# Projection tiles in pairs with seven block products in place of eight, all projections ahead of the mLSTM

## The chip, the cores and the metric

The kernel runs on one core of a Trainium2 chip. The metric is the device time of one execution in microseconds (us). Three runs of the kernel before took 1289.82, 1290.22 and 1290.43 us; their median is 1290.22 us.

## The reference

One layer of a decoder: a sequence of 1024 tokens with 1024 channels, float32, two mixers in parallel that share one input projection.

```python
h = _rmsnorm(x, norm_g)
p = jnp.einsum("bsd,dn->bsn", h, w_in.astype(h.dtype))
q, k, v, o_pre, i_pre, f_pre, z_a, glu_in, z_b, ga_pre, gb_pre = jnp.split(p, SPLIT_POINTS, axis=-1)
qk = jax.nn.silu(_causal_dwconv(jnp.concatenate([q, k], axis=-1), conv_qk_w, conv_qk_b))
...
hm = _mlstm(q.reshape(shp), k.reshape(shp), v.reshape(shp), i_pre, f_pre)
hm = hm * lax.rsqrt(jnp.mean(hm * hm, axis=-1, keepdims=True) + EPS)
hm = hm.reshape(b_, s_, D_A) * mhn_g.astype(jnp.float32)
out_a = (jax.nn.sigmoid(o_pre.astype(jnp.float32)) * hm).astype(x.dtype) * jax.nn.silu(z_a)
y_a = jnp.einsum("bsc,cd->bsd", out_a, w_pa.astype(out_a.dtype))
u = glu_in[..., :D_B] * jax.nn.sigmoid(glu_in[..., D_B:])
u = _causal_dwconv(u, dw_w, dw_b)
u = jax.nn.silu(_layernorm(u, ln_g, ln_b)) * jax.nn.silu(z_b)
y_b = jnp.einsum("bsc,cd->bsd", u, w_pb.astype(u.dtype))
merged = jax.nn.sigmoid(ga_pre) * y_a + jax.nn.sigmoid(gb_pre) * y_b
return x + jnp.einsum("bsd,de->bse", merged, w_out.astype(merged.dtype))
```

The convolution of q and k has 4 taps, that of u has 31. The mLSTM has four heads of 256 channels and goes through the tokens in chunks, with a state that one chunk hands to the next. A last RMSNorm over the channels follows.

## The kernel before

**Products.** A float32 operand is split (`split`, L137) into a high part (a cast on ScalarE) and a low part (a subtraction on VectorE), and `mm3` (L152) adds three matmuls: high by high, high by low, low by high. The weights are the stationary operand. A projection tile (`proj`, L229) has 128 channels by 1024 tokens: two halves of 512 tokens, eight steps along the 1024 input channels, three passes, so 48 matmuls of 512 columns. The projections of w_in are 72 such tiles; v has a form of its own (`v_item`, tokens by 256 channels, one item for each head). y_b, y_a are eight tiles each, and the output projection has 768 matmuls of 256 columns.

**Order.** The program is written as a sequence of items, and a scheduler at build time places each engine's instructions in one fixed list, which the engine then works through in order. First comes the normalised, transposed x (`startup`) with the v of head 0. Then for each head its v, q, k, o (output gate), z_a and four tiles of the gated linear unit, `gb` (its sigmoid is the factor) and `ga`. The mLSTM of a head, four chunks of 256 tokens in six stages each, is laid between the matmuls of the head's last eight tiles (`mlstm_events`). Phase 1b has the merge gates (tiles named sg, first the eight of MB0, then the eight of MA0) and z_b. q, k, v and the gates stay in SBUF until the mLSTM has used them.

**The 31-tap convolution and its layer norm.** `glu_a_item` (L335) forms u and then, at a priority lowered by `LATER`, one start and 30 taps on VectorE over 128x1024 (L341, L344), stores the result in `c_dram` and adds it on GpSimd to `s1`, the sum over channel tiles. `ln_mean` multiplies s1 by a column of ones on TensorE (tstat, L654), and `to_row` transposes the result (trow, L660), writes it to DRAM and loads it back spread over 128 partitions (mu). `ln_var` loads each of the eight tiles c from `c_dram` (ct), subtracts mu, squares, and adds on GpSimd to `sv` (L682); `ln_rstd` and `to_row` give rstd. `d` in the loop of sig_item decides after which sg tile each of these is written: the mean after the first eight, the variance with the next ones. z_b then loads each tile c once more (L673), normalises it, takes the SiLU and multiplies.

**Queues.** All DMAs are issued by SyncE (SP), in order; a store that waits for a result holds up the loads behind it.

## Time and profile before

| | us |
|---|---|
| median of 3 runs | 1290.22 |
| span of the profiled execution | 1287.4 |
| TensorE busy in it | 1275.8 |
| VectorE busy | 816.8 |
| ScalarE busy | 456.6 |
| GpSimd busy | 82.0 |

The profiled execution is known by its span, from its first to its last instruction; the median of the runs stands 2.8 us above it, which is taken for what lies around the span. Matmuls overlap, so the time that a stretch takes is read from the chain of work or from starts, and the mean duration of one matmul (some 0.4 us) is longer than its share of the stretch. The same holds for VectorE: rows that follow one another start closer together than they last.

### The profile page before, as it was taken

Reading aid. Unit: us, or ns where it says so; the run is one execution under the profiler, and the core shown is the slowest. Engines: PE = TensorE matmul, PEld = TensorE weight load, DVE = VectorE, ACT = ScalarE, POOL = GpSimd, SP = SyncE. Lnnn points to the kernel's source line nnn. Section 1 sums busy time; section 2 is a strip of 40 time slices with the busy share of each in tenths; the row PEclk is TensorE's granted clock in tenths of the full one; section 3 lists DMA queues with packets and bytes.
Section 4 is the critical chain, followed back from the end, with each engine's and each line's share of the span. In section 5 each row is a group of like instructions: output and inputs, shape, how many; then the busy total and the mean of one; then the engine's idle time right before and its main releaser. Section 6 shows DMA issues by size and latency. Waiting matters only on the chain.

```text
span 1287.4 us, 16051 instructions
## 1 busy us (share of the span) xinstructions
PE 1275.8 (99%) x6636; PEld 1079.1 (84%) x6636; DVE 816.8 (63%) x1008; ACT 456.6 (35%) x626; POOL 82.0 (6%) x122
## 2 busy tenths in 40 slices
PE   8999999999999999999999999999999999999997
PEld 7888889888889888898888888888888888888997
DVE  6783479995499984799964899262155333344433
ACT  5565441345431444423454211141333211212224
POOL 1000000001000100001010001050000000000002
PEclk9999999999999999999999999999999999999999
DMA  7112121211111221212121123464332344333403
GB/s 219 45 48 53 46 58 42 82 50 58 54 54 50 66 70 37 66 41 66 49 74 50 42 90 115 133 227 127 102 98 82 115 144 137 96 99 98 180 18 132
DMA packets 121495, 109.82 MB, mean 85 GB/s; under 512 B 4945, under 2 KB 109769, under 8 KB 121422
## 3 DMA queue, kind: packets, MB, share of 16 engines
q1 hardware_dynamic: 121422, 108.80, 27.7%
q8 instruction: 52, 0.85, 0.3%
q14 instruction: 21, 0.17, 0.0%
HBM read 87.79 MB, written 21.00 MB: 84 GB/s over the span
## 4 chain that ended last, share of the span: by engine, by line
PE 96%; ACT 1%; DVE 1%; POOL 1%; DMA 0%; issue 0%; SPq 0%; POOLq 0%; ACTq 0%
PE sg L158 14%; PE o L158 7%; PE zb L158 7%; PE k L158 7%; PE ya L158 7%; PE q L158 7%; PE ga L158 7%; PE za L158 7%; PE gb L158 7%; PE yb L158 7%; PE v L158 6%; PE out L158 6%; PE sc L158 2%; PE ip L158 1%; PE up L158 1%; PE np L158 1%
## 5 line engine op out<-in xcount | busy, mean ns | idle before, releaser
L344 DVE SCALAR_TENSOR_TENSOR acc<-u,dww,acc 128x1024 f32<-128x1024 f32 x240 | 307.5, 1307 | 2.9
L138 ACT CAST whi<-wraw 128x1024 fp32r<-128x1024 f32 (+1 forms) x104 | 109.1, 1049 | 372.6 <-PE sg L158 110.6
L139 DVE TENSOR_TENSOR wlo<-wraw,whi 128x1024 fp32r<-128x1024 f32 (+1 forms) x104 | 130.8, 1257 | 78.8 <-ACT whi L138 78.4
L158 PE MATMUL sg<-hth,whi 128*128 128x512 f32 x256 | 101.5, 396 | 0.0
L158 PE MATMUL sg<-hth,wlo 128*128 128x512 f32 x256 | 101.5, 396 | 0.0
L158 PE MATMUL sg<-htl,whi 128*128 128x512 f32 x256 | 100.7, 393 | 0.0
L158 PE MATMUL out<-whi,mrg 128*128 128x256 f32 x512 | 90.8, 280 | 0.0
L158 PE MATMUL ya<-oa,whi 128*128 128x512 f32 x256 | 80.4, 395 | 0.0
L158 PE MATMUL yb<-u,whi 128*128 128x512 f32 x256 | 80.0, 394 | 0.0
L158 PEld LDWEIGHTS out<-whi,mrg 128*128 128x128 f32 x512 | 78.6, 189 | 0.0
L158 PE MATMUL v<-whi,hth 128*128 128x256 f32 (+1 forms) x256 | 71.7, 289 | 2.0 <-ACT hth L138 2.0
L158 PE MATMUL out<-wlo,mrg 128*128 128x256 f32 x256 | 72.0, 281 | 0.0
L158 PE MATMUL v<-whi,htl 128*128 128x256 f32 (+1 forms) x256 | 70.0, 282 | 0.4 <-DVE htl L139 0.4
L158 PE MATMUL v<-wlo,hth 128*128 128x256 f32 (+1 forms) x256 | 69.9, 281 | 0.0
L158 PEld LDWEIGHTS sg<-hth,wlo 128*128 128x128 f32 x256 | 48.3, 189 | 11.9
L158 PEld LDWEIGHTS yb<-u,whi 128*128 128x128 f32 x256 | 48.4, 189 | 11.6 <-DVE u L139 0.3
L158 PEld LDWEIGHTS sg<-htl,whi 128*128 128x128 f32 x256 | 48.0, 187 | 11.7
L158 PEld LDWEIGHTS ya<-oa,whi 128*128 128x128 f32 x256 | 48.0, 188 | 11.4
L158 PEld LDWEIGHTS sg<-hth,whi 128*128 128x128 f32 x256 | 48.1, 188 | 11.0
L158 PE MATMUL ga<-hth,whi 128*128 128x512 f32 x128 | 51.3, 401 | 0.0
L158 PE MATMUL za<-hth,whi 128*128 128x512 f32 x128 | 51.2, 400 | 0.0
L158 PE MATMUL gb<-hth,whi 128*128 128x512 f32 x128 | 50.9, 397 | 0.0
(234 smaller groups left out, 2984.7 us busy)
## 6 DMA issues: line engine op xcount, KB each, us to landing
wraw<-in_w_in_dram SPq DMA_DIRECT2D x80, 512.0 KB, 4.1
ct<-c_dram SPq DMA_DIRECT2D x16, 512.0 KB, 4.6
xt<-in_x_dram SPq DMA_DIRECT2D x8, 512.0 KB, 4.2
oa_dram<-ot SPq DMA_DIRECT2D x16, 256.0 KB, 2.1
c_dram<-acc SPq DMA_DIRECT2D x8, 512.0 KB
sgb_dram<-sg_s SPq DMA_DIRECT2D x8, 512.0 KB, 2.6
sga_dram<-sg_s SPq DMA_DIRECT2D x8, 512.0 KB, 3.0
wraw<-in_w_pb_dram SPq DMA_DIRECT2D x8, 512.0 KB, 4.5
```

The costliest lines, as they stand in the source:

```text
L138: ins = nc.scalar.copy(hi, src)
L139: nc.vector.tensor_tensor(lo, src, hi.bitcast(F32), op=ALU.subtract)
L158: nc.tensor.matmul(ps, a, b, start=(first and j == 0), stop=(last and j == len(todo) - 1))
L344: nc.vector.scalar_tensor_tensor(acc, u[:, k:k + S], dw(k, c), acc, op0=ALU.mult, op1=ALU.add)
```

## The change

Two channel tiles (`jobs`, made by `add`) are computed together. With the two tiles, the two halves of the input channels and the two halves of the tokens, their product is a 2x2 by 2x2 block product, and `quad` forms it with seven block products in place of eight. A block product (`product`) is 128 channels by 512 tokens over 512 input channels: 4 steps and 3 passes, 12 matmuls of 512 columns. So a pair has 84 matmuls where two tiles had 96; there are 36 pairs, jobs 4 to 39, and the four v items are jobs 0 to 3. Of the activations the sums are made once (`sums`); of the weights four block sums are made for each pair (`prep`), and the seven factors are split, seven half tiles where there were four. The partial results X, Z, W in PSUM are copied and added in between by ScalarE and VectorE.

All projections come first. Their results, q and k after the convolution, v, the gates, z_b's product (`u_dram`), go to DRAM. The sums over channel tiles for the layer norm are no longer GpSimd additions but DMAs that add to their destination (`accum_op`), issued by GpSimd: to `s1_dram` in DRAM, and to sv in SBUF. `layer_norm` is written beside jobs 34 and 35, z_b follows as jobs 36 to 39. Then comes the mLSTM, two heads at a time, chunk by chunk, which loads q, k, v and the gate of each chunk; the tiles of y_b are laid between its stages, and y_b loads its input as eight tiles from `u_dram` (`u2_tile`). y_b's product goes to DRAM too (m1_dram) and is loaded for the merge. The buffers of the convolution (u twice, acc once) and the pools that follow share memory that earlier ones must first give up.

```diff
-        def fin():
-            nc.sync.dma_start(c_dram[c], acc)
-            if c == 0:
-                nc.gpsimd.tensor_copy(s1, acc)
-            else:
-                nc.gpsimd.tensor_tensor(s1, s1, acc, op=ALU.add)
-
...
+        a11, a12 = pair("a", raw[:, 1:3])
+        sm = [wq.tile([P, 2, 512], F32, tag="sum", name=f"sum{n}_{i}", bufs=2) for i in range(2)]
+        nc.vector.tensor_tensor(sm[0][:, 0], raw[:, 0], raw[:, 3], op=ALU.add)
+        nc.vector.tensor_tensor(sm[0][:, 1], sm[0][:, 0], raw[:, 1], op=ALU.add)
+        yield
+        s1, s2 = pair("t", sm[0], DMA_LOW)
+        nc.vector.tensor_tensor(sm[1][:, 0], raw[:, 0], raw[:, 1], op=ALU.add)
+        nc.vector.tensor_tensor(sm[1][:, 1], sm[0][:, 1], raw[:, 2], op=ALU.add)
+        yield
+        s3, s4 = pair("s", sm[1], DMA_LOW)
+        yield
+        (a22,) = pair("b", raw[:, 3:4])
+        j["w"] = (a11, a12, s1, s2, s3, s4, a22)
...
+    def sums(tp, ext):
+
+        later = []
+        for k in range(4):
+            r = tp.tile([P, 4, 512], F32, tag="r", name=f"tr{k}")
+            nc.vector.tensor_tensor(r, hb[:, :, 0, k, :].bitcast(F32), hb[:, :, 1, k, :].bitcast(F32), op=ALU.add)
+            t1 = tp.tile([P, 512], F32, tag="t1", name=f"t1_{k}", bufs=4)
+            t3 = tp.tile([P, 3, 512], F32, tag="t3", name=f"t3_{k}")
+            nc.vector.tensor_tensor(t1, r[:, 0], r[:, 2], op=ALU.subtract)
+            nc.vector.tensor_tensor(t3[:, 0], r[:, 3], r[:, 2], op=ALU.subtract)
+            nc.vector.scalar_tensor_tensor(t3[:, 1], t1, -1.0, r[:, 3], op0=ALU.mult, op1=ALU.subtract)
+            nc.vector.scalar_tensor_tensor(t3[:, 2], t3[:, 1], -1.0, r[:, 1], op0=ALU.mult, op1=ALU.subtract)
+            split(ext[:, :, 0, k, :], ext[:, :, 1, k, :], t3)
+            later.append(t1)
+            yield
+        for k in range(4):
+            split(hb[:, 2, 0, k, :], hb[:, 2, 1, k, :], later[k])
...
+    def product(ps, a, b, first, last):
+        for k in range(4):
+            for p, q in PASSES:
+                nc.tensor.matmul(ps, a[p][:, k, :], b[:, q, k, :], start=(first and k == 0 and p == 0 and q == 0),
+                                 stop=(k == 3 and p == 1), skip_group_check=True)
+
+    def quad(n, dst, emit):
+
+        j = jobs[n]
+        bank = lambda name: state["qb"].tile([P, 512], F32, tag="qb", name=f"{name}{n}")
+        ext = state["ext"]
+        b11, b21, t1, b22 = (hb[:, i] for i in range(4))
+        t3, t2, t4 = (ext[:, i] for i in range(3))
+        a11, a12, s1, s2, s3, s4, a22 = j["w"]
+        X, Z = bank("x"), bank("z")
+        product(X, a11, b11, True, False)
+        yield
+        nc.scalar.copy(dst(0, 0), X)
+        product(Z, s1, t1, True, False)
+        yield
+        nc.scalar.copy(dst(1, 1), Z)
+        product(X, s2, t2, False, False)
+        yield
+        nc.scalar.copy(dst(0, 1), X)
+        W = bank("w")
+        product(W, a12, b21, True, True)
+        yield
+        nc.vector.tensor_tensor(dst(0, 0), W, dst(0, 0), op=ALU.add)
+        emit(0, 0, dst(0, 0), False)
+        product(X, s3, t3, False, False)
+        yield
+        nc.vector.scalar_tensor_tensor(dst(1, 1), X, -1.0, dst(1, 1), op0=ALU.mult, op1=ALU.subtract)
+        emit(1, 1, dst(1, 1), False)
+        product(Z, s4, b22, False, True)
+        yield
+        nc.vector.tensor_tensor(dst(0, 1), Z, dst(0, 1), op=ALU.add)
+        emit(0, 1, dst(0, 1), False)
+        product(X, a22, t4, False, True)
+        yield
+        emit(1, 0, X, True)
...
+            acc = cv.tile([P, S], F32, tag="acc", name=f"acc{c}", bufs=1)
+            with tc.high_priority(offset=-LATER):
+                nc.vector.tensor_scalar(acc, u[:, 0:S], dw(0, c), db(c), op0=ALU.mult, op1=ALU.add)
+                for k in range(1, KD):
+                    nc.vector.scalar_tensor_tensor(acc, u[:, k:k + S], dw(k, c), acc, op0=ALU.mult, op1=ALU.add)
+                nc.sync.dma_start(c_dram[c], acc)
+                if c == 0:
+                    nc.sync.dma_start(s1_dram, acc)
+                else:
+                    nc.gpsimd.dma_start(s1_dram, acc, accum_op=ALU.add)
...
+        s1 = lnp.tile([P, S], F32, tag="ct", name="s1", bufs=2)
+        nc.sync.dma_start(s1, s1_dram)
+        ps, st = token_stat(s1, 0)
+        nc.vector.tensor_scalar(st, ps, 1.0 / D, None, op0=ALU.mult)
+        yield
+        to_row(st, 0, mu)
+        yield
+        for c in range(KT):
+            ct = centred(c, 0)
+            if c == 0:
+                nc.scalar.activation(sv, ct, AF.Square)
+            else:
+                nc.scalar.activation(ct, ct, AF.Square)
+                nc.gpsimd.dma_start(sv, ct, accum_op=ALU.add)
+            yield
+        ps, st = token_stat(sv, 1)
+        nc.vector.tensor_scalar(st, ps, 1.0 / D, EPS, op0=ALU.mult, op1=ALU.add)
+        nc.gpsimd.tensor_tensor(st, st, half, op=ALU.pow)
+        yield
+        to_row(st, 1, sv)
...
+    for n in range(4, first_zb - 2):
+        run_job(n)
+    close(cv_cm)
+    ln_cm, state["lnp"] = pool("lnp", reuse_waits="tile")
+    ln = layer_norm()
+    for n in range(first_zb - 2, first_zb):
+        run_job(n, ln)
+    for _ in ln:
+        pass
+    for n in range(first_zb, len(jobs)):
+        run_job(n)
...
+        for i in range(len(chunks) + 2):
+            for f in (at(i - 1, "v"), at(i - 1, "u"), at(i + 2, "l"), at(i, "s"), None, at(i, "k"), at(i + 1, "p"), None,
+                      at(i - 2, "f"), None, at(i, "i")):
+                yield f
...
+    def u2_tile(c):
+        ut = u2p.tile([P, 2, S], F32R, name=f"u2_{c}")
+        raw = yp.tile([P, S], F32, tag="st", name=f"ur{c}", bufs=2)
+        nc.sync.dma_start(raw, u_dram[c])
+        split(ut[:, 0, :], ut[:, 1, :], raw)
+        u2.append(ut)
+
+    def y_b():
+        for d in range(KT):
+            sg = yp.tile([P, S], F32, tag="st", name=f"sgb{d}", bufs=2)
+            nc.sync.dma_start(sg, sgb_dram[d])
+            ps = yield from proj(d, f"yb{d}", rhs=lambda k, sl: (u2[k][:, 0, sl], u2[k][:, 1, sl]))
+            nc.vector.tensor_tensor(sg, ps, sg, op=ALU.mult)
+            nc.sync.dma_start(m1_dram[d], sg)
+
+    chunks[0]["l"]()
+    chunks[1]["l"]()
+    do_load(0)
+    chunks[0]["p"]()
+    yb = y_b()
+    ny = 0
+    last = False
+    for i, f in enumerate(stages()):
+        if f is not None:
+            f()
+        elif i > 22:
+            for _ in range(1 if ny % 8 else 1):
+                next(yb, None)
+                if ny % 8 == 0:
+                    ahead(ny // 8, 1)
+                ny += 1
```

Three places show how this moves instructions in the engines' lists. The first is on TensorE, where the sums for the layer norm (tstat) and their transposes (trow) stand. Before, in the list of merge-gate tiles (sg):

```order
L158 MATMUL sg_6566<-hth,whi_6515 128x512
L158 MATMUL sg_6566<-htl,whi_6515 128x512
L158 MATMUL sg_6566<-hth,wlo_6516 128x512
L654 MATMUL tstat_6624<-ones,s_103 128x2 x8
L158 MATMUL sg_6648<-hth,whi_6573 128x512
L158 MATMUL sg_6648<-htl,whi_6573 128x512
L660 MATMUL trow_6642<-ident,tst_6633 8x128
```

The second sum (tstat from sv) stood 280 rows further on, with sg tiles in between. After, z_6315 is a product of job 39 and z_6180 one of job 38:

```order
L398 MATMUL z_6315<-hb,hi39t 128x512 x2
L398 MATMUL z_6315<-hb,lo39t 128x512
L549 MATMUL tstat_5599<-ones,s_5597 128x2 x8
L555 MATMUL trow_5632<-ident,tst_5608 8x128
L549 MATMUL tstat_5864<-ones,sv 128x2 x8
L555 MATMUL trow_5876<-ident,tst_5873 8x128
L398 MATMUL z_6180<-hb,hi38s 128x512 x2
L398 MATMUL z_6180<-hb,lo38s 128x512
```

Both sums now stand directly behind one another, behind job 38's fifth and job 39's second product; behind them come seven products, the rest of z_b's last two jobs.

The second place is on VectorE, where the last tile's convolution ends (acc). Before:

```order
L344 SCALAR_TENSOR_TENSOR acc_6108<-u_6105,dww,acc_6108 128x1024 x7
L139 TENSOR_TENSOR wlo_6516<-wraw_6403,whi_6515 128x1024
L344 SCALAR_TENSOR_TENSOR acc_6108<-u_6105,dww,acc_6108 128x1024 x6
L139 TENSOR_TENSOR wlo_6574<-wraw_6461,whi_6573 128x1024
L139 TENSOR_TENSOR wlo_6656<-wraw_6519,whi_6655 128x1024
L668 TENSOR_SCALAR tst_6633<-tstat_6624 128x8
L662 COPY rw_6644<-trow_6642 8x128
L139 TENSOR_TENSOR wlo_6723<-wraw_6577,whi_6722 128x1024
L674 TENSOR_TENSOR ct_0_6706<-ct_0_6706,mu 128x1024
L674 TENSOR_TENSOR ct_1_6710<-ct_1_6710,mu 128x1024
```

After, with lo39t a low part of job 39's weights:

```order
L103 TENSOR_TENSOR lo39a<-raw_6162,hi39a 128x1024
L500 SCALAR_TENSOR_TENSOR acc_4980<-u_4825,dww,acc_4980 128x1024
L422 TENSOR_TENSOR f_0_6177<-w_6220,f_0_6177 128x512
L103 TENSOR_TENSOR lo39t<-sum_0_6237,hi39t 128x1024
L500 SCALAR_TENSOR_TENSOR acc_4980<-u_4825,dww,acc_4980 128x1024 x12
L576 TENSOR_SCALAR tst_5608<-tstat_5599 128x8
L557 COPY rw_5634<-trow_5632 8x128
L564 TENSOR_TENSOR ct_0_5658<-ct_0_5658,mu 128x1024
L564 TENSOR_TENSOR ct_1_5680<-ct_1_5680,mu 128x1024
L564 TENSOR_TENSOR ct_2_5704<-ct_2_5704,mu 128x1024
```

The last 12 taps and then the statistics now stand behind job 39's second weight split, and no work of another kind lies among the eight subtractions.

The third place is on TensorE at a pair of the gated linear unit (job 21; job 29 reads alike). Before, an item's last matmuls (here of the last ga tile) were followed by the next item's:

```order
L158 MATMUL ga_6034<-hth,wlo_5928 128x512
L158 MATMUL ga_6034<-hth,whi_5927 128x512
L158 MATMUL ga_6034<-htl,whi_5927 128x512
L158 MATMUL ga_6034<-hth,wlo_5928 128x512
L158 MATMUL sg_6156<-hth,whi_6152 128x512
L158 MATMUL sg_6156<-htl,whi_6152 128x512
```

After, x_4052 is a product of job 23, and z_3720 the sixth of job 21's seven:

```order
L398 MATMUL x_4052<-ext,hi23s 128x512 x2
L398 MATMUL x_4052<-ext,lo23s 128x512
L398 MATMUL x_4052<-ext,hi23s 128x512 x2
L398 MATMUL x_4052<-ext,lo23s 128x512
L398 MATMUL x_4052<-ext,hi23s 128x512
L398 MATMUL z_3720<-hb,hi21s 128x512 x2
L398 MATMUL z_3720<-hb,lo21s 128x512
L398 MATMUL z_3720<-hb,hi21s 128x512 x2
```

Job 21's sixth product has been moved behind the seven of job 22 and the first four of job 23. The copy on ScalarE that it waits for writes u_3717, and the buffer of u_3717 is given up by the convolution of channel tile 3; VectorE's list has that convolution's last tap 35 rows behind job 21's first combination (L422).

## Rows read from the trace of the kernel before

**Rows 1.** The page: span, busy time by engine, granted clock in 40 slices.

```profile
span 1287.4 us, 16051 instructions
...
PE 1275.8 (99%) x6636; PEld 1079.1 (84%) x6636; DVE 816.8 (63%) x1008; ACT 456.6 (35%) x626; POOL 82.0 (6%) x122
...
PEclk9999999999999999999999999999999999999999
```

**Rows 2.** The page's chain that ended last, by engine.

```profile
PE 96%; ACT 1%; DVE 1%; POOL 1%; DMA 0%; issue 0%; SPq 0%; POOLq 0%; ACTq 0%
```

**Rows 3.** The chain in order of time: start us, us, what.

```profile
47.84 22.13 PE q L158 x95
...
204.17 22.65 PE v L158 x192
226.82 22.37 PE q L158 x96
...
897.60 1.68 PE tstat L654 x16
...
1011.40 89.17 PE yb L158 x384
1100.57 89.52 PE ya L158 x384
1190.09 70.84 PE out L158 x600
```

**Rows 4.** Busy time in stretches: stretch, us, engines, clock, DMA share, GB/s.

```profile
206.00:383.00 177.00, 177.00 (x943) 150.81 (x942) 142.46 (x175) 70.36 (x96) 10.00 (x19) 1.00 0.20 57
```

**Rows 5.** VectorE in order of time: start us, us, instructions.

```profile
209.97 8.46 DVE L344 SCALAR_TENSOR_TENSOR acc<-u,dww,acc 128x1024 f32<-128x1024 f32 x7
218.34 1.22 DVE L139 TENSOR_TENSOR vl<-v,vh 128x1024 fp32r<-128x1024 f32 x1
219.48 8.46 DVE L344 SCALAR_TENSOR_TENSOR acc<-u,dww,acc 128x1024 f32<-128x1024 f32 x7
...
241.95 4.06 DVE L310 SCALAR_TENSOR_TENSOR qraw<-qpre,par,qraw 128x511 f32<-128x511 f32 x6
245.92 1.28 DVE L344 SCALAR_TENSOR_TENSOR acc<-u,dww,acc 128x1024 f32<-128x1024 f32 x1
...
1111.80 1.29 DVE L753 TENSOR_TENSOR sga<-ya,sga 128x512 f32<-128x512 f32 x2 [8.84 <-PE ya L158]
1113.01 1.28 DVE L754 TENSOR_TENSOR sga<-sga,m 128x512 f32<-128x512 f32 x2
```

**Rows 6.** VectorE, ScalarE and GpSimd around the layer norm's statistics, in order of time.

```profile
830.96 0.28 DVE L662 COPY rw<-trow 8x128 f32<-8x128 f32 x1 [0.52 <-PE trow L660]
...
839.46 2.36 DVE L674 TENSOR_TENSOR ct<-ct,mu 128x1024 f32<-128x1024 f32 x2 [7.09 <-DMA mu<-mu_dram]
...
899.56 2.57 POOL L687 TENSOR_TENSOR tst<-tst,half 128x8 f32<-128x8 f32 x1 [30.41 <-DVE tst L686]
...
919.09 1.28 ACT L714 ACT_TABLE_LOAD   x1 [6.73 <-DVE ct L713]
```

**Rows 7.** The tile ct: durations min/median/max in ns; time to landing of its loads.

```profile
L674 DVE TENSOR_TENSOR ct<-ct,mu x16: 1211/1226/3419, 839.5 to 987.8; 128x1024 f32<-128x1024 f32 x16
...
L714 ACT ACTIVATE ct<-ct,par x8: 1225/1243/1245, 920.4 to 990.4; 128x1024 f32<-128x1024 f32 x8
...
L680 ACT ACTIVATE ct<-ct x7: 1050/1060/1062, 843.5 to 865.5; 128x1024 f32<-128x1024 f32 x7
L682 POOL TENSOR_TENSOR sv<-sv,ct x7: 2395/2407/3267, 844.7 to 866.7; 128x1024 f32<-128x1024 f32 x7
...
DMA to landing us min/median/max: 3.2/4.6/5.3
```

**Rows 8.** Time to landing of the stores of sg_s, 512 KB each.

```profile
DMA to landing us min/median/max: 2.6/2.8/3.2
```

**Rows 9.** The last stretch, as in rows 4; the last matmul ends at 1280.7.

```profile
1286.00:1287.40 1.40, 0.00 (x0) 0.00 (x0) 0.00 (x0) 0.00 (x0) 0.00 (x0) 0.50 0.00 0
```

More of the change, by code (lines that the diff above doesn't have):

```diff
@@ new lines, with token_stat @@
+    for i in range(4):
+        add(f"gb{i}", lambda n: act_job(n, AF.Sigmoid, keep="sg"), GB0_, i)
+        add(f"ga{i}", lambda n, i=i: glu_job(n, 2 * i), GA0_, i)
+        for name, fn, base, h in rest[6 * i:6 * i + 6]:
+            add(f"{name}{h}", fn, base, h)
+    first_zb = len(jobs)
+    for i in range(4):
+        add(f"zb{i}", lambda n, i=i: zb_job(n, i), ZB0, i)
+    def token_stat(acc, n):
+        ps = ms(f"tstat{n}")
+        for t in range(TT):
+            nc.tensor.matmul(ps[:, 2 * t:2 * t + 2], acc[:, t * P:(t + 1) * P], ones, start=True, stop=True)
+        st = state["lnp"].tile([P, TT], F32, name=f"tst{n}")
+        return ps[:, 0:2 * TT].rearrange("p (t o) -> p t o", o=2)[:, :, 0:1].rearrange("p t o -> p (t o)"), st
@@ new lines, in zb_job, with run_job @@
+    def zb_job(n, i):
+        cts = []
+        for j in range(2):
+            ct = centred(2 * i + j, 1)
+            nc.vector.tensor_tensor(ct, ct, state["rstd"], op=ALU.mult)
+            nc.scalar.activation(ct, ct, AF.Silu, bias=lb(2 * i + j), scale=lg(2 * i + j))
+            cts.append(ct)
+        return act_job(n, AF.Silu, store=lambda j: u_dram[2 * i + j], by=lambda j: cts[j])
+    def run_job(n, *others):
+        load(n + 1)
+        side = [prep(n + 1) if n + 1 < len(jobs) else iter(()), *others]
+        for step, _ in enumerate(jobs[n]["fn"](n)):
+            if step > 1:
+                for g in side:
+                    next(g, None)
+        for _ in side[0]:
+            pass
@@ new lines, with start @@
+    st_cm, st_pool = pool("st_pool", reuse_waits="tile")
+    warm = ms("warm")
+    for _ in range(11):
+        nc.tensor.transpose(warm[:, 0:P], ident, ident)
+    state["st"] = st_pool
+    gen = startup(st_pool)
+    def start(t):
+        next(gen, None)
+        if t == 4:
+            load_params(st_pool)
+    state["start"] = start
+    start(0)
+    start(1)
+    run_job(0)
+    close(st_cm)
+    gate_steps = gates()
+    next(gate_steps)
+    run_job(1)
+    next(gate_steps, None)
+    close(vt_cm)
@@ new lines, in do_split, with ahead, proj @@
+    def do_split(i):
+        if i < len(slots) and i not in done:
+            do_load(i)
+            done.add(i)
+            hi, lo = [wpool.tile([P, KT * P], F32R, tag=x, name=f"{x}{i}", bufs=3) for x in ("whi", "wlo")]
+            split(hi, lo, raws.pop(i))
+            splits[i] = (hi, lo)
+    def ahead(i, n):
+        for j in range(i, i + n + 1):
+            do_split(j)
+        do_load(i + n + 1)
+    def proj(i, name, rhs):
+        do_split(i)
+        wv = [v.rearrange("p (k c) -> p k c", k=KT) for v in splits.pop(i)]
+        ps = pj(name)
+        for hf in range(2):
+            sl = slice(hf * 512, (hf + 1) * 512)
+            pairs = [((wv[0][:, k, :], wv[1][:, k, :]), rhs(k, sl)) for k in range(KT)]
+            for k in range(0, KT, 2):
+                mm3(ps[:, sl], pairs[k:k + 2], first=k == 0, last=k == KT - 2)
+                yield
+        return ps
@@ L632, in run @@
+    while todo:
+        oa_tile(todo.pop(0))
     def run(gen, i):
```

693 lines of the change are left out of this document (331 added, 362 removed).

## The prediction

> **What bounds the kernel now.** I read the page first, then the chain, then the stretch of one head. TensorE is busy 99% at full granted clock [rows 1] and holds 96% of the chain that ended last [rows 2]; no other engine has more than 1%. So nothing is waited for, and time is a count of matmuls. The chain in order of time gives the price: 96 matmuls of 512 columns, one q item, take 22.37 us, 0.2331 us each; a v item takes 22.65 [rows 3]. In the stretch of head 1 (an item for v and seven more items, 206 to 383) VectorE is busy 142.5 of 177 us [rows 4]: 80%, the engine that stands next. The layer norm's statistics, a sequence of stalls between VectorE, GpSimd and DMAs, lie beside sg matmuls and cost TensorE 1.7 us [rows 3, 6].
>
> **What is removed.** A product is 12 x 0.2331 = 2.80 us, a pair 84 x 0.2331 = 19.58 for 22.38. 36 pairs save 36 x 2.80 = 100.7 us. On TensorE alone the new program would be:
> - start (the first q chain ends at 69.98, less its 22.38) 47.6;
> - three v items at 22.6: 67.8;
> - 36 pairs: 704.9;
> - the mLSTM, which is what is left of the span: 1287.4 - 47.6 - 36 x 22.38 - 67.8 - (89.17 + 89.52) - 97.3 = 90.3, less 4.5 for the startup's gate transposes and the layer norm's two sums, which I count elsewhere: 86;
> - y_b and y_a 178.7; from the end of y_a (1190.09) to the end of the span 97.3 [rows 3].
>
> This makes 1182, and with about 4 us of waiting for the gates' transposes (VectorE's `sums` now stand ahead of them; estimated as seven VectorE operations at 0.6) 1186. Job 4 then starts at 47.6 + 67.8 + 4 = 119.4.
>
> **VectorE in the pairs.** Its price is read from starts that follow one another: a tap (209.97 to 218.34 for seven) 1.196, a subtraction of 1024 (218.34 to 219.48) 1.14, 512 columns 0.605 (1111.80 to 1113.01 for two), 512 columns of the other form 0.66 (241.95 to 245.92 for six) [rows 5]. A pair's weights take three subtractions of 1024, one of 512 and four sums of 512; its results two combinations of the first form and one of the second: 3.42 + 0.60 + 2.42 + 1.21 + 0.66 = 8.3. Eight jobs (q, k, o, z_a, two glu, two merge gates) take 66.4, two convolutions of 31 taps 74.2, twelve taps for q and k 14.4, two products of gates 2.3, four halves of u 2.4: 159.7 us, where TensorE wants 8 x 19.58 = 156.6. The saving thus uses up VectorE's reserve: it is full, and the convolution, which stands at low priority, is late wherever it is waited for.
>
> **Where that is waited for: two glu pairs.** At job 21 (and 29) the sixth product stands behind a copy into a buffer of u that the convolution of channel tile 3 (5) gives up. VectorE has ahead of it, from job 21's first combination, 21 taps (25.1), six taps of q and k (7.2), five subtractions of 1024 (5.7), twelve operations of 512 (7.2): 45.2, and the copy 0.6. TensorE has 12 products laid between, 33.6. It stands 45.8 - 33.6 = 12.2 us; twice: 25 us in round figures. (At job 13 the same count gives 22 us of VectorE against 25 of TensorE: nothing.) These stalls also pay for VectorE's excess of 3.1 us in each of the 4.25 groups of eight.
>
> **The layer norm, the large term.** 34 pairs and four products of job 38 end at 119.4 + 665.7 + 11.2 + 25 = 821.3. Then VectorE has a combination, a subtraction and the last 12 taps (14.4): the convolution ends at 837.4. TensorE has done its seven products ahead of tstat by 119.4 + 665.7 + 19.6 + 25 = 829.7. There it stands, in its fixed list, and the seven products behind it can't pass. The chain:
> - the DMA that adds to s1. No DMA of this kind is in the trace. Nearest rows: a store of 512 KB lands in 2.6 to 3.2 us [rows 8], a load of ct in 3.2 to 5.3 [rows 7]. An addition has to read and write, so I take a load's median, 4.6; bounds 2.6 (a plain store) and 9.2 (two passes). It ends at 842.0; the load of s1, 4.6, at 846.6;
> - tstat 1.7 [rows 3], its scaling 0.2, trow 0.5; from the copy of the row to the first use of mu 8.5 (830.96 to 839.46) [rows 6]: 857.5;
> - the variance. Before, GpSimd's additions of 2.4 us in SBUF stood here [rows 7]; now DMAs, with two buffers of ct. Two subtractions 2.4, a square 1.06 and an addition 4.6 make 8.1 for the first two tiles; then three rounds of load 4.6 + 1.2 + 1.06 + 4.6 = 11.5: 42.6, ends at 900.1. Bounds: 30 with additions of 2.6 and loads of 3.2; 68 with additions of 9.2, which then follow one another: 12.7 + 6 x 9.2;
> - tstat 1.7, scaling 0.2, GpSimd's power 2.57, trow 0.5, row to rstd 8.5 [rows 6]: 913.6;
> - restart: TensorE's sixth product of job 38 waits for a buffer that z_b's first tile gives up: normalising 1.14, the table load 1.28, SiLU 1.24, a product 1.14, store 2.8, copy 0.6 [rows 5 to 8] = 8.2: 921.8. TensorE has stood 92 us, about as much as the seven-product form saves.
>
> Of that standing the last row shows what follows: with the last matmul at 1280.7 the granted clock from 1286 is 0.50, the lower of the two levels [rows 9]. I add 3 us, one product at half speed. Products: 921.8 + 19.6 + 3 = 944.4.
>
> The Trainium skill, "DMA: Bandwidth & Descriptors", "Anatomy of one DMA — SWDGE (gpsimd) path", gives for a DMA issued by GpSimd 2.0 us plus the bytes over 436 GB/s, by which 512 KB would take an estimated 3.2 us, the loop 37 us, and the sum would be 1322; no run so far shows whether it holds for a DMA that adds.
>
> **After it.** z_b's eight tiles go through two buffers, four rounds of load 4.6 and four passes, about 9 each: the last product's store is ready 36 us behind rstd. In SP's list it stands ahead of the loads of y_b's input (eight, in two buffers: 4.6 + 1.06 + 1.14, four rounds, 27): y_b can begin at 913.6 + 36 + 27 = 977. TensorE has about four mLSTM chunks before that (16 chunks in 86 us: 5.4 each, 22): 944.4 + 22 = 966, so 11 to 12 us are lost. In the rest, TensorE's work of a chunk depends on copies and factors; uncovered, one such pass of ScalarE and one of VectorE (1.06 + 0.6) would cost 27 us over 16 chunks, covered by the other head's chunk and y_b nothing; I take 8.
>
> **The sum.** 944.4 + 86 + 178.7 + 97.3 + 12 + 8 = 1326.4, and 2.8 us by which the median stands above the profiled span: **1329 us**, 3.0% above 1290.22. A measurement of this kernel can tell 0.2% from no change.
>
> **Rivals.**
> - **TensorE stays the bound (faster).** For it: before, the same statistics cost 1.7 us. It needs the convolution to end some 85 us before TensorE reaches tstat; then the 92 + 3 us vanish: 1234 (without the glu stalls and those after it, 1189). Against: VectorE's list holds the last 12 taps directly ahead of the statistics, and the count above gives it no reserve. It decides at an end of the convolution near 745; near 795 it would be equal. Chance 0.10.
> - **VectorE bounds all pairs.** If operations cost what they last (tap 1.28, 1024 columns 1.22, 512 columns 0.64 [rows 5]), eight jobs take 171 against 156.6 plus the glu stalls' share of 5.9: 8.3 x 4.25 = 35 us more, 1364. Against: rows that follow one another do start closer. Chance 0.10.
> - **The mLSTM phase waits throughout**, at its upper bound and with one load's latency more in each pair of chunks: 19 + 8 x 2.6 = 40 more, 1369. Against: two heads take turns. Chance 0.06.
> - **The clock stays low** through all seven products after the stand: 19.6 - 3 more, 1346. The last row shows the fall, no row a recovery. The Trainium skill, "TensorE: Matmul & The Clock Gate", "Part 1: The HAM clock gate", calls half clock the default that activity releases; rows 9 agree with the first half. Chance 0.04.
>
> **How the numbers follow.** The forecast has 0.70. Its cheap end: variance loop 30 (-12), addition to s1 2.6 (-2), one glu stall less (-12), no loss after (-20): 1283. Its dear end: loop 68 (+25), addition to s1 9.2 (+5), the mLSTM's bound (+19): 1378. The range leaves out the first rival and the corner of the cheap end, and takes in the others: 1288 to 1380. Faster: 0.10 from the first rival and 0.04 from the cheap corner; same 0.04; slower 0.82.
>
> **What would show it.** Products at 2.80 us and a pair at 19.6; VectorE over 90% busy until the convolution ends; about 12 us of waiting for a ScalarE copy at jobs 21 and 29, nothing at 13; TensorE idle some 90 us around the two tstat, ended by DMAs that add, VectorE and mu's way through DRAM; a second hole of some 10 us before y_b; TensorE busy near 1180 in all. I am wrong if a DMA that adds takes far from 4.6 us (seven of them stand in a row), if the convolution ends tens of us earlier, or if the mLSTM with y_b between its stages stalls by more than 30 us.

## The result, and the profile after

The changed kernel takes 1388.53 us (median of 4 runs, 1385.22 to 1390.03) where the kernel before took 1290.33 beside it: 1.0759 times, 95% interval 1.0743 to 1.0774. The forecast had the sign and the place of the largest loss, but 1329 us, with a range to 1380. The profiled execution spans 1383.5 us where the sum of the prediction gave 1326.4; this is how the 57.1 us between them lie, each end of a stretch read from TensorE's list in order of time:

| stretch | sum of the prediction | trace | more |
|---|---|---|---|
| start, to job 4 | 119.4 | 123.5 | 4.1 |
| job 4 to the last product ahead of tstat | 710.3 | 721.2 | 10.9 |
| TensorE's stand at the two tstat, to the restart | 92.1 | 95.1 | 3.0 |
| seven products behind it | 22.6 | 22.2 | -0.4 |
| mLSTM with y_b | 195.2 | 217.5 | 22.3 |
| y_a to the end | 186.8 | 204.0 | 17.2 |

Where the 4.1 us at the start come from was not looked for. The page of after, to set beside [rows 1, 2]; the chain's line is short here, since the chain was followed back only to 1032 us:

```profile
span 1383.5 us, 16366 instructions
...
PE 1212.9 (88%) x6204; PEld 1017.5 (74%) x6204; DVE 1031.0 (75%) x1322; ACT 552.0 (40%) x844; POOL 56.5 (4%) x157
...
PEclk9999999999999989999899997557799999899999
...
PE 15%; DMA 3%; DVE 3%; ACT 2%; POOL 1%; issue 1%; SPq 0%; POOLq 0%; ACTq 0%; DVEq 0%
```

TensorE is busy 63 us less and the span is 96 us longer: it no longer sets the time alone. Stretches of after, columns as in [rows 4]:

```profile
123.50:844.70 721.20, 690.17 (x2940) 554.18 (x2940) 657.71 (x691) 299.94 (x389) 6.13 (x12) 0.99 0.31 90
844.70:939.80 95.10, 7.94 (x36) 7.16 (x35) 28.59 (x28) 11.41 (x11) 8.57 (x9) 0.53 0.49 132
939.80:962.00 22.20, 22.20 (x84) 17.67 (x84) 16.93 (x17) 9.76 (x13) 0.00 (x0) 0.87 0.44 145
962.00:1000.00 38.00, 22.52 (x114) 19.49 (x114) 30.81 (x52) 30.14 (x55) 2.44 (x17) 0.73 0.91 292
1000.00:1179.50 179.50, 167.46 (x1009) 145.90 (x1009) 123.06 (x284) 86.43 (x195) 20.34 (x81) 0.99 0.62 196
1179.50:1206.00 26.50, 17.54 (x48) 9.43 (x48) 11.97 (x10) 8.08 (x8) 0.00 (x0) 0.81 0.61 198
```

In the first, the pairs, VectorE is busy 657.7 of 721.2 us (91%, where it had 80% in [rows 4]) and TensorE stands 31 us. The second is the stand. In the fourth, the mLSTM's first 38 us, TensorE works for 22.5 of them at a mean clock of 0.73. TensorE around the stand, in order of time (start, us; in brackets the idle time ahead and what ended it):

```profile
865.80 3.57 PE L549 MATMUL tstat<-ones,s 128*128 128x2 f32 x16 [21.07 <-DMA s<-s_dram]
...
921.27 3.58 PE L549 MATMUL tstat<-ones,sv 128*128 128x2 f32 x16 [51.27 <-DMA sv<-ct]
926.87 0.37 PE L555 MATMUL trow<-ident,tst 128*8 128x128 f32 x1 [2.02 <-POOL tst L590]
939.78 1.22 PE L398 MATMUL z<-hb,hi38s 128*128 128x512 f32 x2 [12.55 <-ACT f L415]
```

And VectorE: the first tap of three convolutions, the weight split ahead of one of them, and the last taps of the last one.

```profile
268.53 1.22 DVE L103 TENSOR_TENSOR lo12a<-raw,hi12a 128x1024 fp32r<-128x1024 f32 x1 [5.61 <-ACT hi12a L102]
271.64 0.81 DVE L498 TENSOR_SCALAR acc<-u,dww,par 128x1024 f32<-128x1024 f32 x1 [1.89 <-DMA s_dram<-acc]
...
623.57 0.81 DVE L498 TENSOR_SCALAR acc<-u,dww,par 128x1024 f32<-128x1024 f32 x1 [7.24 <-DMA s_dram<-acc]
...
797.37 0.81 DVE L498 TENSOR_SCALAR acc<-u,dww,par 128x1024 f32<-128x1024 f32 x1 [7.00 <-DMA s_dram<-acc]
...
840.04 15.81 DVE L500 SCALAR_TENSOR_TENSOR acc<-u,dww,acc 128x1024 f32<-128x1024 f32 x12
```

The last convolution ends at 855.8 (forecast 837.4). A tile's first tap waits for the DMA that adds the tile before it to s1, since acc has one buffer: 18.4 us over four convolutions. At 268.5 and 447.2 VectorE also waited 5.6 and 3.6 us for a cast, as no tap was left in its list between the end of one tile and the first tap of the next: 27.6 us with these. No term of the prediction had either wait.

### The profile page after: what moved, and what is told of

The parts are those of the page before. It is cut to its first block, busy times and chain, and to the rows that moved or that the text cites. A ratio compares the mean times of both kernels' runs of the same rounds, so it can differ in the third digit from the quotient of the medians.

```text
span 1383.5 us, 16366 instructions
## 1 busy us (share of the span) xinstructions
PE 1212.9 (88%) x6204; PEld 1017.5 (74%) x6204; DVE 1031.0 (75%) x1322; ACT 552.0 (40%) x844; POOL 56.5 (4%) x157
## 5 line engine op out<-in xcount | busy, mean ns | idle before, releaser
L112 PE MATMUL v<-hi,hb 128*128 128x256 f32 (+1 forms) x512 | 95.0, 288 | 2.6 <-ACT hb L102 2.1
L112 PEld LDWEIGHTS v<-hi,hb 128*128 128x128 f32 x512 | 79.9, 192 | 3.7 <-ACT hb L102 2.7
L112 PE MATMUL v<-lo,hb 128*128 128x256 f32 (+1 forms) x256 | 71.6, 288 | 0.0
L448 ACT ACTIVATE f<-f 128x512 f32<-128x512 f32 x72 | 45.3, 632 | 57.5 <-DVE f L426 31.6
L470 DVE SCALAR_TENSOR_TENSOR qa<-qr,par,qa 128x1023 f32<-128x1023 f32 (+2 forms) x48 | 60.0, 1276 | 0.0
L102 ACT CAST whi<-wr 128x1024 fp32r<-128x1024 f32 x24 | 25.2, 1049 | 78.1 <-PE ya L112 57.4
L112 PE MATMUL ya<-oa,wlo 128*128 128x512 f32 x128 | 51.5, 402 | 0.0
L112 PE MATMUL yb<-u,wlo 128*128 128x512 f32 x128 | 50.9, 398 | 0.0
L112 PEld LDWEIGHTS out<-wlo,mrg 128*128 128x128 f32 x256 | 49.1, 192 | 0.0
L112 PEld LDWEIGHTS v<-lo,hb 128*128 128x128 f32 x256 | 48.6, 194 | 0.0
```

What stands on the lines that cost most here:

```text
L102: ins = nc.scalar.copy(hi, src)
L112: nc.tensor.matmul(ps, a, b, start=(first and j == 0), stop=(last and j == len(todo) - 1))
L448: nc.scalar.activation(t[j][:, HF[hf]], src, func, scale=sgn(neg))
L470: nc.vector.scalar_tensor_tensor(acc[j][:, s:], raw[j][:, 0:S - s], cw(KQ - 1 - s, t), acc[j][:, s:], op0=ALU.mult, op1=ALU.add)
```

## The experiments

They ran in five groups (e1 to e4, e5 to e8, e9 to e12, e13 to e16, e17 and e18), the kernels of a group on one chip with the kernel before; a ratio is to the kernel before, with its 95% interval.

| run | us | ratio |
|---|---|---|
| the change | 1388.5 | 1.0759 [1.0743, 1.0774] |
| e1_acc2 | 1350.1 | 1.0465 [1.0448, 1.0483] |
| e2_low_by_dma | 1342.1 | 1.0404 [1.0388, 1.0419] |
| e3_eight_products | 1353.1 | 1.0501 [1.0467, 1.0534] |
| e4_oa_buffers | 1381.5 | 1.0713 [1.0697, 1.0729] |
| e5_one_pass | 1340.9 | 1.0393 [1.0376, 1.0411] |
| e6_early_loads | 1350.7 | 1.0467 [1.0451, 1.0483] |
| e7_lows_on_gpsimd | 1358.4 | 1.0527 [1.0511, 1.0543] |
| e8_yb_behind | 1368.5 | 1.0605 [1.0583, 1.0628] |
| e9_one_pass_short | 1301.8 | 1.0090 [1.0072, 1.0108] |
| e10_sums_on_gpsimd | 1378.1 | 1.0681 [1.0659, 1.0703] |
| e11_all_hidden | 1351.2 | 1.0467 [1.0443, 1.0492] |
| e12_low_by_dma_all | 1330.9 | 1.0318 [1.0285, 1.0352] |
| e13_glu_sooner | 1330.3 | 1.0309 [1.0293, 1.0324] |
| e14_glu_sooner_two | 1322.4 | 1.0245 [1.0225, 1.0265] |
| e15_lows_half | 1324.4 | 1.0264 [1.0247, 1.0281] |
| e16_stores_on_gpsimd | 1298.6 | 1.0066 [1.0050, 1.0082] |
| e17_squares_own_buffer | 1295.5 | 1.0038 [1.0025, 1.0051] |
| e18_squares_two_sooner | 1293.4 | 1.0031 [1.0019, 1.0042] |

**What holds the convolution up: its buffer.**

```diff
-            acc = cv.tile([P, S], F32, tag="acc", name=f"acc{c}", bufs=1)
+            acc = cv.tile([P, S], F32, tag="acc", name=f"acc{c}", bufs=2)
```

> The convolution's result gets two buffers (acc, 2 for 1). Theory: VectorE is full and the layer norm's chain begins where the last convolution ends; after's trace shows VectorE idle 1.9, 2.3, 7.2 and 7.0 us at the first tap of a convolution, until the DMA that adds the last result to s1 has landed. Without this wait the last tap ends up to 18 us earlier than 855.8, TensorE's stand of 95 us begins and ends that much earlier or shrinks, and the kernel takes 1370 to 1380 for 1388.5. Rival: VectorE has slack elsewhere or the list only shifts, and the time stays within 3 us of 1388.5.

One buffer more takes 38 us off, twice the most that was expected. TensorE in that run, in order of time:

```profile
826.77 3.58 PE L549 MATMUL tstat<-ones,s 128*128 128x2 f32 x16 [14.34 <-DMA s<-s_dram]
...
882.65 3.58 PE L549 MATMUL tstat<-ones,sv 128*128 128x2 f32 x16 [51.67 <-DMA sv<-ct]
...
901.19 1.22 PE L398 MATMUL z<-hb,hi38s 128*128 128x512 f32 x2 [12.57 <-ACT f L415]
```

The chain from the first tstat on is as it was (74.4 us to the restart, 74.0 in the change). All of the gain lies ahead of it: the last tap ends at 817, TensorE is there at 812.4 for 844.7, and the stalls in jobs 23 and 31 are gone (no wait of more than 1.3 us between job 4 and tstat). In the change they were 7 us each, and what stood there was a buffer of another kind:

```profile
508.91 1.22 PE L398 MATMUL x<-ext,hi23t 128*128 128x512 f32 x2 [7.09 <-ACT qr L412]
```

The copy into qr had waited for the store of a q result, that is for VectorE's taps of q (ScalarE in the change):

```profile
503.14 1.28 ACT L472 ACT_TABLE_LOAD   x1 [5.80 <-DVE qa L470]
...
508.27 0.58 ACT L412 COPY qr<-x 128x512 f32<-128x512 f32 x1 [1.65 <-DMA q_dram<-qa]
```

So VectorE was late in the pairs too, and not only at the end. But the edit does more than end the waits at the first taps: with two buffers the scheduler lays the two convolutions of a pair beside one another, and VectorE's list is another. In e1 the second tile's first tap stands 4.4 us behind the first tile's:

```profile
162.07 0.81 DVE L498 TENSOR_SCALAR acc<-u,dww,par 128x1024 f32<-128x1024 f32 x1
...
166.43 0.81 DVE L498 TENSOR_SCALAR acc<-u,dww,par 128x1024 f32<-128x1024 f32 x1
```

In the change it stands at 271.64, behind all 31 of the first. At job 21's first weight split VectorE has done 93 operations of the convolution in the change and 103 in e1; up to there, and to the first tap behind it, the change had lost 13.4 us between tiles, 4.2 of them at first taps. That the one buffer costs 38 us is shown; how much of it is waiting and how much the order that the buffer forces on the list, no run separates.

**The order alone, and VectorE's load.** e3 forms each pair with eight products: its quad is

```diff
+        for t, hf in ((0, 0), (1, 1), (0, 1), (1, 0)):
+            X = bank(f"x{t}{hf}_")
+            product(X, w[t][0], bb[2 * hf], True, False)
+            yield
+            product(X, w[t][1], bb[2 * hf + 1], False, True)
+            yield
+            nc.scalar.copy(dst(t, hf), X)
+            emit(t, hf, dst(t, hf), False)
```

without the sums of weights and activations.

> The order of the change alone: each pair by eight block products as before (96 matmuls for 84), no sums of activations or weights, results copied by ScalarE. Theory: TensorE has 36 x 2.80 = 101 us more, VectorE per pair some 5 us less, so the convolution keeps ahead, the 95 us at the tstat and the 31 us of stalls in the pairs go, and what the order costs is left: the waits in the mLSTM with y_b (about 42 us over the matmuls) and ahead of y_a (15): 1340 to 1350, that is 50 to 60 more than before. Rival: the stand at tstat belongs to the order (all projections first), not to VectorE's load: 1430 or more.

It takes 1353.1, 8 us over the middle of what was expected: all of the change but the seven products costs 63 us, and these add 35 to that. The stalls in the pairs go, but not the whole stand: the two tstat still wait 9.5 and 14.7 us. VectorE between 297 and 471, e3 and then the change:

```profile
297.00:471.00 174.00, 174.00 (x770) 144.06 (x769) 115.67 (x105) 65.05 (x91) 1.97 (x4) 1.00 0.31 91
```

```profile
297.00:471.00 174.00, 170.73 (x736) 137.08 (x735) 164.81 (x174) 74.03 (x97) 2.19 (x4) 1.00 0.34 97
```

66% busy against 95%, and TensorE without a gap against 3.3 us of gaps. Beside e1, which has two acc buffers, the seven products seem to bring 3 us of their 101 (1350.1 to 1353.1), but the two intervals overlap, and eight products with two buffers were not run.

e2 sets the kernel's switch `DMA_LOW`, by which ScalarE and an adding DMA form two of four low parts:

> Two of a pair's four weight splits form their low part with ScalarE and a DMA that adds (the switch DMA_LOW that the kernel has), which takes 2 x 1.14 = 2.3 us per pair off VectorE, 78 us in 34 pairs. Theory (VectorE full, convolution late): the convolution ends near 780, the stalls in jobs 23 and 31 go, the stand at the two tstat falls from 95 to some 55 us, and the kernel takes 1300 to 1330. Rival: such a DMA takes 5.4 to 6.0 us in after's trace, so weights come late for their product and TensorE waits in every pair: 1380 or more.

1342.1: 46 us less, not 58 or more as expected. The last tap ends at 798.8, but TensorE waits some 18 us in the pairs, most of it for combinations that VectorE does late, and later once for such a DMA itself. VectorE in turn waits 13.8 us for acc, which has one buffer here, and 53.6 us over the whole run for buffers of sums that such DMAs still read. One wait of TensorE of either kind:

```profile
426.06 1.22 PE L398 MATMUL x<-ext,hi18b 128*128 128x512 f32 x2 [2.95 <-DVE f L426]
...
851.96 0.80 PE L398 MATMUL z<-hb,lo39t 128*128 128x512 f32 x1 [7.51 <-DMA lo39t<-sum]
```

**The chain of the layer norm.** e5 takes the variance from sums of squares, so the second pass goes:

```diff
+                sq = u[:, 0:S]
+                nc.scalar.activation(sq, acc, AF.Square)
...
+                    nc.gpsimd.dma_start(s2_dram, sq, accum_op=ALU.add)
```

> On top of the two acc buffers (1350.1 us): the variance is taken as mean of squares less squared mean. ScalarE squares each convolution's result as soon as it is there (into the buffer of u that it frees), a DMA adds it to a second sum, and the second pass over the eight stored tiles goes. Theory: the stand at the two tstat (826.8 to 901.2 in that run) is a chain of latencies, 55 us of it the loop of load, subtraction, square and adding DMA; without the loop the restart comes 45 to 55 us earlier and the time is 1295 to 1305. Rival: the kernel is bound elsewhere meanwhile (y_b's input, z_b's tiles), so part of the gain is given back: 1310 to 1335.

1340.9, above even what the rival named. From the last tap to the restart it takes 38 us for 84, as the theory had it; but the last tap is at 857.8 again, because u is held until its squares are added, and TensorE waits at the copies into u, in jobs 13, 21 and 29, three waits of 4.9 to 9.1 us and two shorter ones. The longest:

```profile
661.16 1.22 PE L399 MATMUL x<-ext,hi29t 128*128 128x512 f32 x2 [9.06 <-ACT u L413]
```

This is the kind of stall that the prediction had counted for the change, and it appears when it is u that is short. Place and size agree in part: jobs 21 and 29 lose 7.8 and 12.5 us, where 12.2 each were counted, but at the sixth product only 5.0 and 3.5 of them, and job 13, where nothing was counted, loses 4.9. e9 squares the first six tiles on GpSimd in quarters, in a buffer of its own (and has e4's buffers):

> On top of the two acc buffers (1350.1 us): the single pass for the variance again, but the squares no longer hold a buffer of u: for the first six tiles GpSimd squares quarters in a buffer of their own, only the last two tiles use u. Also the three buffers for y_a's loads (worth 7 us). Theory: in the run before, the chain behind the last tap fell from 84 to 38 us, and 42 us were lost ahead of it because u was held; with u free both gains stay: 1350 - 46 - 7 = 1297, range 1290 to 1305. Rival: squares on GpSimd beside VectorE slow the taps, which are the bound: 1315 or more.

1301.8, inside the range and 5 us over the sum. Both gains stay: TensorE is at tstat at 819 and restarts at 860.0. GpSimd's squares, 26.0 us in all, leave the taps at 1286 ns on average, so the rival's condition did not come.

**Ahead of y_a.** e4:

```diff
-        raw = yp.tile([P, S], F32, tag="st", name=f"oar{d}", bufs=2)
+        raw = oap.tile([P, S], F32, tag="oar", name=f"oar{d}", bufs=3)
```

> The eight loads of the mLSTM's result for y_a get three buffers of their own in place of two that they share. Theory: y_a's first matmuls wait for a chain load 3.7, cast 1.05, subtraction 1.24 that goes through two buffers four times (1179.5 to 1205, 15 us lost); with three the chain is shorter by a third: 1380 to 1385. Rival: the loads wait for the last chunk's store to oa_dram or for y_b's end, not for buffers: within 2 us of 1388.5.

7 us less: the chain of loads through two buffers was 7 of the 17 us lost there. What SP issues there in the change (start, us) shows where more of it lies:

```profile
1180.65 0.33 SPq L891 DMA_DIRECT2D m_dram<-sgb  x1
1181.79 0.33 SPq L920 DMA_DIRECT2D oar<-oa_dram  x1
```

Seven of the eight loads (oar) stand behind the store of y_b's last tile, and that store waits for the product, which ends with y_b. Whether this costs the rest was not tried by itself.

**The mLSTM phase.** Its matmuls would take 175 us by the prediction's sum (86 + 89), and it takes 217.5. Four runs looked for the cause.

> On top of the two acc buffers (1350.1 us): the first q and k tiles of the mLSTM lie in memory that the weight sums give up, no longer in that of the last products' operands, and their loads stand in GpSimd's queue. Theory: after the last product TensorE waits 11 us for load, cast and subtraction, because the first buffers of the mLSTM share memory with operands of the last product; with the loads landed before, 4 to 5 us are left: 1342 to 1346. Rival: the wait comes from the casts behind other work on ScalarE and VectorE (z_b's last tiles), and the time stays at 1348 to 1352.

No change (1350.7), but this run doesn't test what it was made for. GpSimd's list has the mask's memset ahead of the loads, and that waited for the last product:

```profile
923.12 0.31 POOL L680 MEMSET mask<- 128x256 f32 x1 [34.59 <-PE x L398]
923.68 0.80 POOL L740 DMA_DIRECT2D q<-q_dram  x1 [0.25 <-issue]
```

So the loads started when the products were over, as before, and the first score waited 8.8 us for 11.0 in e1. What loads that are really early would bring stays open. In the change the wait is for ScalarE's cast of k, behind z_b's last SiLU and a table load:

```profile
969.21 1.24 ACT L600 ACTIVATE ct<-ct,par 128x1024 f32<-128x1024 f32 x1 [1.38 <-DVE ct L599]
970.47 1.28 ACT L751 ACT_TABLE_LOAD   x1
971.76 0.52 ACT L751 ACTIVATE dm<-dm 128x384 f32<-128x384 f32 x1
972.23 0.62 ACT L102 CAST kh<-k 128x512 fp32r<-128x512 f32 x1
```

> On top of the two acc buffers (1350.1 us): the low parts of k and v in the mLSTM are subtracted on GpSimd, 32 operations of 0.6 us that VectorE no longer does. Theory A: VectorE's list, 79% busy and on nearly every step of the chain there, sets the pace of the mLSTM with y_b between its stages, which takes 217 us for 175 us of matmuls: 8 to 15 us less, 1335 to 1342. Theory B: loads behind stores in SP's queue and the clock set the pace: within 3 us of 1350, or slower, since GpSimd takes about twice as long for one.

8 us slower: VectorE's work is not what sets the pace there, or GpSimd's longer operations cost more than they free; the run doesn't tell which.

> On top of the two acc buffers (1350.1 us): no matmuls of y_b between the mLSTM's stages; y_b runs behind it as a whole, and the loads for y_a lie beside it. Theory (VectorE's work of 8 to 9 us per chunk bounds the 16 chunks): the mLSTM alone takes 135 to 150 us, y_b 90, and the 15 us ahead of y_a go: 1345 to 1365. Rival: the mLSTM alone is a chain of latencies that y_b fills well: 170 us and more, 1380 or over.

18 us slower, a little more than expected, and less clear than meant: the scheduler still drew matmuls of y_b (from 951.6 on) between the stages.

> On top of the best so far (1301.8 us): the stores of the mLSTM's result and of y_b stand in GpSimd's queue, so that loads no longer stand behind stores that wait for results in SP's. Theory (SP's order costs the mLSTM phase its waits; there SP waits 29 us for gate results, 29 for such stores to land, 24 for y_b's): 1285 to 1295. Rival (loads are two chunks ahead and land in time; the phase loses by the first chunk's casts, the clock and the chain of stages): 1299 to 1305.

1298.6 for e9's 1301.8, on another chip; the ranges of the runs touch (1296.8 to 1300.9, 1300.4 to 1303.2). SP's order is worth about 3 us at most. So the phase has no single cause among those tried. What the trace of the change shows of its 42 us: 27.5 are waits of TensorE (10.7 of them the first score), some 8 the lower clock (an estimate from 22.5 us of work at 0.73, the rest nearly at 1), and the remaining 7 are not accounted for.

**GpSimd and DMAs in VectorE's place.** e10 makes the four weight sums of a pair on GpSimd:

> On top of the two acc buffers (1350.1 us): the four weight sums of a pair are made on GpSimd, not on VectorE (4 x 0.6 us per pair, 82 us in 34 pairs). Theory (VectorE's load puts the convolution's end behind TensorE): the last tap ends some 40 us or more before 817, the mean's tstat stands inside job 37, and the stand shrinks by as much: 1305 to 1320. Rival: GpSimd takes about twice as long and slows VectorE while both run, or the sums come too late for their splits: 1340 or more.

28 us slower than e1. Groups of that run by line (busy us, mean ns):

```profile
L500 DVE SCALAR_TENSOR_TENSOR acc<-u,dww,acc 128x1024 f32<-128x1024 f32 x240 | 356.8, 1517 | 1.0
...
L199 POOL TENSOR_TENSOR sum<-sum,raw 128x512 f32<-128x512 f32 x36 | 76.1, 2114 | 2.7
```

A tap lasts 1517 ns on average for 1279 in e1, and GpSimd takes 2.1 us for what VectorE did in 0.68. So 57 us of the 82 freed come back in the taps, and other operations slow too, most of all the weight splits of 512 columns (1480 ns on average for 689): from job 4 to tstat VectorE is busy 666.9 us, where it was 657.0 in e1. The Trainium skill, "SBUF — State Buffer", "SBUF: two separate sides", says that a VectorE operation with two inputs in SBUF and a GpSimd operation that reads SBUF exclude each other at a shared pair of ports, for a whole instruction. The tap is such an operation, and the trace agrees: 76 of the 240 taps last 2.0 us on average, the median is 1275 ns as ever.

> Both: the single pass with GpSimd's squares, the weight sums on GpSimd, two acc buffers, three for y_a's loads. Theory: the convolution ends early enough and the chain behind it is 38 us, so TensorE does not stand at the tstat at all; of after's 1388.5 the 25 to 31 us in the pairs, the 95 of the stand and 7 ahead of y_a go: 1255 to 1270, faster than before. Rival: GpSimd now has squares, sums and the adding DMAs in one list and is late with one of them: 1290 or more.

1351.2: the same contention (a tap 1544 ns), the rival's side. e12 has e2's switch in place of GpSimd's sums:

> As the run before, but with the low parts of two splits formed by ScalarE and a DMA that adds in place of the sums on GpSimd. Theory: VectorE is freed alike (2.3 us per pair), but in the run with this switch alone TensorE waited 20 us in the pairs for results behind them and 7.5 for one such DMA: 1280 to 1295. Rival: the DMAs that add queue up behind the squares on GpSimd, and pairs wait: over 1320.

1330.9, also the rival's side: VectorE waits up to 9.9 us at a time for a sum's buffer that such a DMA still reads. e15 uses the switch for one split of the four, together with glu pairs one job sooner:

> As the glu pairs one job sooner, and one of a pair's four splits (that of the last sums, used last) forms its low part with ScalarE and a DMA that adds: 1.14 us per pair less on VectorE, 39 us in 34 pairs. Theory: the convolution ends near TensorE's arrival or ahead of it, the chain of 38 us is mostly hidden: 1270 to 1285. Rival: as with two such splits the DMAs' latency costs TensorE about what VectorE gains: 1295 or more.

1324.4, the rival's side again, with the same waits of VectorE, up to 9.3 us at a time.

**Glu pairs sooner.**

```diff
-        for name, fn, base, h in rest[6 * i:6 * i + 6]:
+        for name, fn, base, h in rest[(0, 5, 11, 17, 24)[i]:(0, 5, 11, 17, 24)[i + 1]]:
```

> On top of the best so far (1301.8 us: two acc buffers, single pass for the variance, three buffers ahead of y_a): the second to fourth glu pairs stand one job sooner (jobs 11, 19, 27 for 12, 20, 28). Theory (the convolution's end, set by VectorE's load, stands behind TensorE): VectorE had about 30 us without work while only one glu pair was there, so the last tap ends up to 20 us sooner and the stand of 46 us at the tstat shrinks by as much: 1282 to 1295. Rival: VectorE is full from job 12 on, u is then not free for the sooner pair and the stall moves into the pairs: 1300 or more.

> As the run before, but the third and fourth glu pairs stand two jobs sooner (18, 26). Theory: the convolution's end would come up to 40 us sooner, yet seven jobs of 19.6 us leave VectorE less time than two convolutions need, so part is paid in stalls at the copies into u: 1275 to 1295. Rival: all of it is paid there: 1300 or more.

1330.3 and 1322.4, slower than e9 by 28 and 21. VectorE waits for acc again, which GpSimd's squares now hold (22.3 us at three first taps in e13):

```profile
517.52 0.81 DVE L499 TENSOR_SCALAR acc<-u,dww,par 128x1024 f32<-128x1024 f32 x1 [8.98 <-POOL sqc L514]
```

e17 and e18 take these two orders of jobs again, with e16's stores, and give the squares a buffer of their own on ScalarE; its room comes from half-width buffers for the splits that are half as wide:

```diff
+        if tag == "b":
+            return [wq.tile([P, 512], F32R, tag=x + tag, name=f"{x}{n}{tag}", bufs=1) for x in ("hi", "lo")]
...
+                sq = cv.tile([P, S], F32, tag="sqc", name=f"sqc{c}", bufs=1)
+                nc.scalar.activation(sq, acc, AF.Square)
```

> Glu pairs one job sooner again, now with the squares on ScalarE into a buffer of their own (room from the half-width splits, which used full-width buffers), so that neither u nor acc is held by them; also the stores in GpSimd's queue. Theory: in the earlier run with sooner pairs VectorE waited 6.7 to 9.0 us at three first taps for acc, which GpSimd's squares held; without that the convolution ends some 15 us sooner than in the best so far (1298.6): 1272 to 1288, at or just below before's 1290. Rival: u is the buffer that is short with the pairs closer together: 1295 or more.

> As the run before with the third and fourth pairs two jobs sooner. Theory: the convolution ends up to 20 us sooner still, but VectorE has seven jobs (137 us) for two convolutions (74) and seven pairs' own work (65), nothing to spare, so 5 to 15 us of it come back as stalls at u: 1268 to 1288. Rival: the stalls take all: 1295 or more.

1295.5 and 1293.4. Both miss their range, e17 on the rival's side and e18 between the two, and the best of all is still 0.3% above the kernel before. In e18 the stand is gone, since both tstat lie among products (the first waits 2.5 us), and what is left is elsewhere: a wait for u in a glu pair, and the mLSTM with y_b.

```profile
447.50 0.79 PE L401 MATMUL x<-ext,hi19t 128*128 128x512 f32 x1 [12.46 <-ACT u L415]
```

```profile
881.00:1096.00 215.00, 191.53 (x1121) 166.85 (x1122) 148.65 (x327) 109.71 (x240) 38.37 (x114) 0.94 0.64 208
```

36 pairs take 745 us (123.8 to 869.1) for 705 of products, and 227 us pass from there to y_a (1095.8) for 175 of matmuls. With 17 at the start and from y_a on this is 109 us over the sum of TensorE's work (1182 in the prediction), and 101 is what the seven products save.

## Why the prediction was wrong, point by point

- **The products** were right: the stretch to 844.7 has 690.2 us of work for 685.3 counted, with the lower clock behind the stalls. "A pair 84 x 0.2331" holds. TensorE's busy time in all, "near 1180", was 1212.9, about half of the excess in the mLSTM with y_b (190.0 for 175, at a mean clock of 0.95).
- **VectorE is full** was right (91 to 95% busy), and e3 shows that it is the seven products that fill it.
- **The two glu stalls** did not come: nothing waits for u at jobs 21 and 29 in the change. TensorE waited 7.1 us each at jobs 23 and 31 instead, for the copy into qr, and that all waits in the pairs make 31 us for the 25 counted is luck. The step counted VectorE's rows up to the release of u and took them to follow one another. What broke the row was acc's one buffer: the waits at first taps, for the adding DMA, and a list in which one tile's taps stand behind all of another's. e1 shows that the buffer did it, by taking the stalls away with u unchanged; e5 shows that the wait for u comes when u is held.
- **The end of the convolution**, "837.4", was 855.8: 18 us late, for the same missing term, which was put at nothing; without it (e1) the kernel is 38 us faster.
- **The layer norm's chain**, 84.4 us from the last tap to the restart, measured 83.9; single terms were off both ways. (Before, the two tstat cost TensorE 1.7 us each, and not 1.7 in all.) The adding DMAs landed in

```profile
DMA to landing us min/median/max: 4.6/5.4/5.6
```

to SBUF and 6.0 us to DRAM (median), for 4.6 taken; the loop took 44.6 for 42.6, the way of rstd 11.3 for 13.5. By the page of the Trainium skill cited in the prediction ("DMA: Bandwidth & Descriptors", "Anatomy of one DMA — SWDGE (gpsimd) path") it would have been an estimated 3.2: its fit did not hold for these DMAs that add.
- **The mLSTM with y_b**, "12 + 8", was the step that failed by most: 20 us counted over the matmuls, 42 measured. The sum took the loss from y_b's late input, put the start of the phase at nothing and let it begin at once. The first score waits 10.7 us for its load and its cast behind z_b's last work on ScalarE; y_b began at 986.5 (977 forecast); the clock was lower meanwhile. Together with shorter waits these are some 35 us of the 42; what sets the pace of the phase stays open. The rival "the mLSTM phase waits throughout", 1369, had 0.06 and came nearest to the time; whether by its mechanism, a load's latency and two uncovered passes in the chunks, no run shows.
- **From y_a to the end** nothing was added, without a reason, and it cost 17: y_a's input is loaded, cast and split after y_b has ended, 7 us of it through two buffers (e4). The sum priced the boundary at the layer norm and neither of the other two.
- **The range** summed its dear end to 1378 over the layer norm and the mLSTM alone; the pairs and y_a had no dear end at all.
- **The rival "TensorE stays the bound"** fell: even with the stand removed (e18) the time is 1293.4, not 1234, since the order costs as much as the products save.

## What to carry to other kernels

A saving on the engine that bounds uses up the reserve of the next one; from then on each buffer that is given up late delays everything behind it, so the count of a full engine's rows must include the wait for every buffer that its next block writes. A buffer that a DMA still reads is held for the DMA's whole time, and a single one also fixes the order of the work that writes it: a second one was worth 38 us here. And when one long interleaved stretch is cut into phases, price each boundary: what TensorE has to do while the first loads, casts and table loads of the next phase run.
